# Moving 30 gathered expert rows from the second output projection and retrieval to the one-hot stage

## The chip, the cores and the metric

One core of a Trainium2 chip. The metric is the device time of one execution in microseconds, as the median of several runs. Differences of about 0.2% (5.5 us) and less can't be told from no change.

## What is computed

One layer of a hybrid encoder on 1024 tokens of width 1024, in float32: a mixing part (differential attention and a gated linear recurrence) with an output projection, and then PEER, a product-key retrieval of single-neuron experts, which this change concerns:

```
h = h + mix @ w_out
xt = rmsnorm(h, norm2_g)
q = (xt @ w_query).reshape(T, 8, 2, 128)
v1, i1 = top_k(q[:, :, 0] @ keys_1.T, 16); v2, i2 = top_k(q[:, :, 1] @ keys_2.T, 16)
sc, ci = top_k(v1[..., :, None] + v2[..., None, :], 16)
eid = i1[ci // 16] * 128 + i2[ci % 16]        # 8 heads x 16 = 128 experts for each token
act = gelu(einsum('thkd,td->thk', expert_down[eid], xt))
h = h + einsum('thk,thkd->td', softmax(sc) * act, expert_up[eid])
out = rmsnorm(h, norm_f_g)
```

There are 128 x 128 = 16384 experts, and each has a row of 1024 numbers in `expert_down` and one in `expert_up`.

## The kernel before

The tokens are cut into 8 blocks of 128. The first three (NG = 3) get their experts by **gathering rows**: for each of the 128 slots of a block GpSimd starts an indirect DMA that fetches one expert row for each of the 128 tokens (line 878, 512 KB in all), and VectorE takes it in with one instruction, for `expert_down` a product and sum against x2g (line 895), for `expert_up` a weighted addition to accg (line 905). That makes 3 x 2 x 128 = 768 rows. A row lands in one of five buffers of the pool `rows`, so a gather waits until the instruction that read its buffer is done. Line 728 at last scales a finished block.

The other five blocks (ND = 5) are **dense**: TensorE multiplies them by all of `expert_down` (`down_all`, tiles pd), the weights of the chosen experts are spread by one-hot matrices (`one_hots`, line 1135, and `weights`, tiles pg), and TensorE multiplies by all of `expert_up` (tiles pu); VectorE adds the sums to acc (line 1260), and the end norms the five blocks (lines 1266, 137 to 142 and 728).

After the first three blocks have chosen their experts, the program runs these stages: attention for the dense blocks; the second output projection (`for i in range(ND)`: two times eight matmuls into pa, line 997, an addition of x into h on VectorE, line 999, the square on ScalarE, line 1002, the multiplication to xt, line 1003, a reciprocal root of small instructions, a diagonal matrix diag, line 1006, and `turn`, which transposes and scales the block, line 982, and splits it into xdH and xdL, lines 126 and 127); the second retrieval (`query`, with `top_k_g` for the gathered blocks 1 and 2 beside it, index addition in line 932); a top-k for each dense block; the one-hot matrices; and the up stage.

The gathered rows are a generator, `gathered()`, and a stage takes steps of it by `gather_steps`. How many, the table G_ATT, G_OUT, G_QRY, G_TOPK, G_OH and G_UP says, and G_UP is what is left of 768:

```
gather_steps(G_OUT / (ND - G_LAST) if i < ND - G_LAST else 0)   # each block of the projection
gather_steps(G_QRY / (2 * PH))                                  # each of 16 query columns
gather_steps(G_OH * TB / (TD - OH_LAST) if t0 < TD - OH_LAST else 0)
gather_steps(G_UP / (n_steps - LAST))                           # each expert block of the up stage
gather_steps(2 * NG * SLOTS + 1)                                # what is left
```

This sets only where the steps stand in the program. The order on each engine is made when the program is built, by a planner that works out when each instruction could start and puts them in that order; row instructions are kept in their own order (`tc.keep_in_program_order`), and so are a few others. On the chip each engine then runs its list from first to last.

Of the kernel before, what the change touches and what calls it, by code (L numbers as in the profile page):

```python
# [47 lines left out]
TB = 16  # L48
TI = 2

G_ATT, G_OUT, G_QRY, G_TOPK, G_OH = 64, 24, 46, 0, 168
G_UP = 2 * NG * SLOTS - (G_ATT + G_OUT + G_QRY + G_TOPK + G_OH)
B_OUT, B_CHAIN, B_TURN, B_QRY, B_TOPK = 0, 3, 8, 8, 12
A_STEPS, A_AHEAD, A_FILL, LRU_AT, WO_AT = 3, 4, 0.5, 0.7, 50
# [1270 lines left out]
```

## Time and profile before

| | |
|---|---|
| median of 3 runs | 2761.29 us (2756.67 to 2762.64) |
| the profiled execution | 2766.01 us, its span 2764.2 us |
| TensorE (PE) busy | 2629.9 us, 95% of the span |
| VectorE (DVE) busy | 2274.7 us, 82% |
| ScalarE (ACT) busy | 1199.2 us, 43% |
| GpSimd (POOL) busy | 1093.7 us, 40% |
| DMA | 795.75 MB, 288 GB/s in the mean |

The span goes from the first to the last record of the profile, and the execution's own time is 1.8 us longer. Engines work side by side, so the shares don't add up to 100%. An instruction is named by its line, its output and its inputs, with buffer numbers left out.

### The profile page before, as it was taken

What the parts mean: (1) busy time and instruction counts of PE and PEld (TensorE: products, weight loads), DVE (VectorE), ACT (ScalarE), POOL (GpSimd) and SP (SyncE); (2) the same over time, 40 slices, a digit from 0 to 9 for tenths busy, and PEclk for the clock granted to TensorE, in tenths of its full rate; (3) what the DMA queues carried; (4) which work ended last, traced back from release to release, by engine and by line L of the source; (5) the groups of instructions that cost most, each with busy time, mean ns of one, the idle gap of its engine ahead of it and who ended that gap; (6) DMA issues with size and microseconds to landing.
All of it is one profiled execution on the core that took longest, in us unless ns stands there. A gap on an engine that the chain in (4) does not pass through costs nothing.

```text
span 2764.2 us, 43413 instructions
## 1 busy us (share of the span) xinstructions
PE 2629.9 (95%) x15577; PEld 2325.0 (84%) x15577; DVE 2274.7 (82%) x4737; ACT 1199.2 (43%) x2549; POOL 1093.7 (40%) x938
## 2 busy tenths in 40 slices
PE   7989978889999899999999999999999999999996
PEld 6767965746999899999998888888888888888885
DVE  6554879977999979998976788888888888888898
ACT  6653437632324657888862222222223222222222
POOL 2110236544231005443323455445444545545454
PEclk9989989989999999999999999999999999999998
DMA  6556999878684339999999999999999999999987
GB/s 194 139 134 205 319 208 267 240 262 300 213 285 147 115 128 336 358 348 330 340 373 335 324 336 321 342 333 355 337 332 339 341 331 327 346 345 326 349 295 260
DMA packets 321321, 795.75 MB, mean 288 GB/s; under 512 B 26208, under 2 KB 126576, under 8 KB 318544
## 3 DMA queue, kind: packets, MB, share of 16 engines
q0 software_dynamic: 141040, 442.44, 48.1%
q1 hardware_dynamic: 163248, 283.81, 30.4%
q10 hardware_dynamic: 16816, 66.72, 6.0%
q8 instruction: 122, 2.00, 0.3%
q14 instruction: 95, 0.78, 0.1%
HBM read 690.77 MB, written 102.11 MB: 287 GB/s over the span
## 4 chain that ended last, share of the span: by engine, by line
PE 77%; DVE 8%; DMA 7%; issue 4%; ACT 3%; POOL 1%; DVEq 0%; SPq 0%; ACTq 0%; POOLq 0%
PE pu L158 10%; PE pu L161 10%; PE pu L162 10%; PE pd L158 10%; PE pd L162 10%; PE pd L161 9%; PE pg L1159 4%; PE pa L158 3%; PE pa L162 2%; PE pa L161 2%; DMA row<-in_expert_up,eid 2%; PE pp L158 1%; PE pp L162 1%; PE pp L161 1%; PE pa L605 1%
## 5 line engine op out<-in xcount | busy, mean ns | idle before, releaser
L878 POOL DMA_INDIRECT row<-in_expert_up,eid x384 | 503.7, 1312 | 679.2 <-DVE accg L905 552.3
L878 POOL DMA_INDIRECT row<-in_expert_down,eid x384 | 492.7, 1283 | 570.0 <-DVE row L895 463.5
L158 PE MATMUL pd<-xdH,dh 128*128 128x320 f32 x2048 | 639.2, 312 | 3.7 <-ACT dh L126 3.3
L162 PE MATMUL pd<-xdH,dl 128*128 128x320 f32 x2048 | 631.5, 312 | 11.2 <-DVE dl L127 11.2
L161 PE MATMUL pd<-xdL,dh 128*128 128x320 f32 x2048 | 634.5, 310 | 0.0
L905 DVE SCALAR_TENSOR_TENSOR accg<-row,wg,accg 128x1024 f32<-128x1024 f32 x384 | 491.1, 1279 | 26.0 <-DMA row<-in_expert_up,eid 23.7
L161 PE MATMUL pu<-ul,w_h 128*128 128x512 f32 x1280 | 502.7, 393 | 1.0 <-DVE ul L127 1.0
L162 PE MATMUL pu<-uh,w_l 128*128 128x512 f32 x1280 | 498.5, 391 | 0.0
L895 DVE SCALAR_TENSOR_TENSOR row<-row,x2g 128x1024 f32<-128x1024 f32 x384 | 461.3, 1217 | 31.8 <-DMA row<-in_expert_down,eid 29.9
L162 PEld LDWEIGHTS pd<-xdH,dl 128*128 128x128 f32 x2048 | 385.6, 189 | 19.4 <-DVE dl L127 12.3
L158 PE MATMUL pu<-uh,w_h 128*128 128x512 f32 x1280 | 390.6, 393 | 9.5 <-DVE acc L1260 3.5
L158 PEld LDWEIGHTS pd<-xdH,dh 128*128 128x128 f32 x2048 | 387.4, 189 | 12.0 <-ACT dh L126 3.6
L161 PEld LDWEIGHTS pd<-xdL,dh 128*128 128x128 f32 x2048 | 387.2, 189 | 7.7
L126 ACT CAST uh<-uraw 128x512 fp32r<-128x512 f32 x256 | 157.9, 620 | 493.3 <-PE pu L162 395.8
L161 PEld LDWEIGHTS pu<-ul,w_h 128*128 128x128 f32 x1280 | 241.2, 188 | 49.0 <-DVE ul L127 2.2
L158 PEld LDWEIGHTS pu<-uh,w_h 128*128 128x128 f32 x1280 | 237.1, 189 | 53.1 <-issue 6.9
L162 PEld LDWEIGHTS pu<-uh,w_l 128*128 128x128 f32 x1280 | 240.6, 188 | 47.8
L126 ACT CAST dh<-draw 128x512 fp32r<-128x512 f32 x256 | 158.0, 618 | 248.9 <-PE pd L161 232.1
L127 DVE TENSOR_TENSOR ul<-uraw,uh 128x512 fp32r<-128x512 f32 x256 | 175.2, 686 | 73.9 <-ACT uh L126 72.4
L127 DVE TENSOR_TENSOR dl<-draw,dh 128x512 fp32r<-128x512 f32 x256 | 175.5, 686 | 71.9 <-ACT dh L126 67.1
L1146 ACT ACTIVATE o1a<-o,slot_a 128x128 bf16<-128x128 bf16 x640 | 194.4, 428 | 1.1 <-DVE o L1135 0.8
L126 ACT CAST w_h<-ga 128x640 fp32r<-128x640 f32 x128 | 93.0, 729 | 231.0 <-PE pu L161 138.3
(284 smaller groups left out, 4107.2 us busy)
## 6 DMA issues: line engine op xcount, KB each, us to landing
draw<-in_down_t SPq DMA_DIRECT2D x128, 512.0 KB
uraw<-in_up_h SPq DMA_DIRECT2D x128, 512.0 KB
gw<-gw_d SPq DMA_DIRECT2D x32, 1280.0 KB
gw_d<-st ACTq DMA_DIRECT2D x20, 1536.0 KB
act<-ga ACTq DMA_DIRECT2D x70, 320.0 KB
ga<-act SPq DMA_DIRECT2D x70, 320.0 KB
w_d<-w POOLq DMA_DIRECT2D x32, 512.0 KB
w<-w_d SPq DMA_DIRECT2D x32, 512.0 KB
```

The source lines that it names most:

```text
L126: A.copy(hi, src)
L127: (eng or V).tensor_sub(lo, src, hi.bitcast(F32))
L158: t = T.matmul(ps, wh, mh, start=first, stop=False)
L161: T.matmul(ps, wh, ml, start=False, stop=False)
L162: T.matmul(ps, wl, mh, start=False, stop=last)
L605: T.matmul(pss[:, t - t0, :], qt[:, t * P:(t + 1) * P], kt[:, ct % 2, :], start=True, stop=True)
L878: nc.gpsimd.indirect_dma_start(out=r, out_offset=None, in_=table, in_offset=bass.IndirectOffsetOnAxis(ap=eids[tb][:, s:s + 1], axis=0))
L895: tc.keep_in_program_order(V.scalar_tensor_tensor(r, r, 1.0, x2, op0=ALU.mult, op1=ALU.mult, accum_out=act[:, s:s + 1]))
L905: tc.keep_in_program_order(V.scalar_tensor_tensor(acc, r, w[:, s:s + 1], acc, op0=ALU.mult, op1=ALU.add))
L1146: A.activation(oa[:, g, :, j], o[:, g, 1, :, j], AF.Copy, scale=slot_a[b][:, tt + t:tt + t + 1])
L1159: T.matmul(ps[:, t - t4, :], o[:, g, 0, :, j], part[:, g, :, j], start=i == 0, stop=i == 2)
```

## The change

```
-G_ATT, G_OUT, G_QRY, G_TOPK, G_OH = 64, 24, 46, 0, 168
+G_ATT, G_OUT, G_QRY, G_TOPK, G_OH = 64, 0, 40, 0, 198
```

The 24 steps of the projection and 6 of the 46 steps of the queries go to the one-hot matrices. G_UP stays 466, and nothing else is edited. The order on the engines is made anew. Three places of it follow.

VectorE in the second output projection, around a block's two additions to h (line 999); L905 takes in a gathered row, n_v, n_r and n_t are the reciprocal root. Before:

```order
L999 TENSOR_TENSOR h<-pa,xt_5869 128x512
L905 SCALAR_TENSOR_TENSOR accg<-row,wg,accg 128x1024
L142 SCALAR_TENSOR_TENSOR n_r<-n_t,n_r 128x1
L905 SCALAR_TENSOR_TENSOR accg<-row,wg,accg 128x1024
L141 SCALAR_TENSOR_TENSOR n_t<-n_r,n_v 128x1
L905 SCALAR_TENSOR_TENSOR accg<-row,wg,accg 128x1024
L142 SCALAR_TENSOR_TENSOR n_r<-n_t,n_r 128x1
L905 SCALAR_TENSOR_TENSOR accg<-row,wg,accg 128x1024
L141 SCALAR_TENSOR_TENSOR n_t<-n_r,n_v 128x1
L142 SCALAR_TENSOR_TENSOR n_r<-n_t,n_r 128x1
L1006 TENSOR_SCALAR diag<-ident,n_r 128x128
L905 SCALAR_TENSOR_TENSOR accg<-row,wg,accg 128x1024
```

The same block in the change:

```order
L999 TENSOR_TENSOR h<-pa,xt_5819 128x512 x2
L1003 TENSOR_TENSOR xt_5819<-h,g2b 128x1024
L137 TENSOR_SCALAR n_v<-ss_5842 128x1
L138 TENSOR_SCALAR n_r<-n_v 128x1
L141 SCALAR_TENSOR_TENSOR n_t<-n_r,n_v 128x1
```

The row instructions between the block's own are gone.

VectorE at the first one-hot matrices with rows beside them (o and o1v are the matrices, dl a split of expert weights). Before:

```order
L1135 TENSOR_TENSOR o_10697<-key_t,slot_k_8428 128x4096
L127 TENSOR_TENSOR dl<-draw,dh 128x512
L905 SCALAR_TENSOR_TENSOR accg<-row,wg,accg 128x1024 x2
L127 TENSOR_TENSOR dl<-draw,dh 128x512
L905 SCALAR_TENSOR_TENSOR accg<-row,wg,accg 128x1024
L127 TENSOR_TENSOR dl<-draw,dh 128x512
L1139 TENSOR_TENSOR o1v<-o_10697,slot_w_8433 128x4096
```

The same in the change:

```order
L1135 TENSOR_TENSOR o_10614<-key_t,slot_k_8336 128x4096
L127 TENSOR_TENSOR dl<-draw,dh 128x512
L895 SCALAR_TENSOR_TENSOR row,actg<-row,x2g 128x1024 x5
L127 TENSOR_TENSOR dl<-draw,dh 128x512 x2
L1139 TENSOR_TENSOR o1v<-o_10614,slot_w_8341 128x4096
```

Here five rows stand in place of three, and they are earlier rows of the stream (`expert_up` rows before, `expert_down` rows now).

VectorE at the end, behind the third of the five last additions of TensorE's sums (line 1260, acc_16753 to acc_16757). Before:

```order
L1260 TENSOR_TENSOR acc_16755<-acc_16755,pu 128x512
L905 SCALAR_TENSOR_TENSOR accg<-row,wg,accg 128x1024 x2
L1260 TENSOR_TENSOR acc_16756<-acc_16756,pu 128x512
L905 SCALAR_TENSOR_TENSOR accg<-row,wg,accg 128x1024
L1260 TENSOR_TENSOR acc_16757<-acc_16757,pu 128x512
L1266 TENSOR_TENSOR ss_27911<-ssd 128x1
```

The same in the change:

```order
L1260 TENSOR_TENSOR acc_16755<-acc_16755,pu 128x512
L905 SCALAR_TENSOR_TENSOR accg<-row,wg,accg 128x1024 x2
L1260 TENSOR_TENSOR acc_16756<-acc_16756,pu 128x512
L905 SCALAR_TENSOR_TENSOR accg<-row,wg,accg 128x1024
L1260 TENSOR_TENSOR acc_16757<-acc_16757,pu 128x512
L905 SCALAR_TENSOR_TENSOR accg<-row,wg,accg 128x1024 x26
L1266 TENSOR_TENSOR ss_27911<-ssd 128x1
```

Between the last addition and the norms (line 1266) now stand 26 row instructions, where there was none.

## Rows read from the trace of the kernel before

**Rows 1.** The page's busy times, whole span (us, share, instructions).

```profile
PE 2629.9 (95%) x15577; PEld 2325.0 (84%) x15577; DVE 2274.7 (82%) x4737; ACT 1199.2 (43%) x2549; POOL 1093.7 (40%) x938
```

**Rows 2.** Busy time by stretch: length, engines (instructions), granted clock, DMA share, GB/s.

```profile
620.00:680.00 60.00, 56.97 (x217) 35.39 (x216) 49.34 (x85) 14.79 (x25) 30.02 (x25) 0.94 0.84 300
680.00:870.00 190.00, 188.59 (x1325) 188.32 (x1324) 175.72 (x892) 54.98 (x110) 47.13 (x37) 1.00 0.62 218
870.00:957.00 87.00, 78.14 (x519) 76.88 (x519) 85.24 (x428) 49.61 (x85) 11.68 (x10) 0.96 0.48 158
957.00:1417.00 460.00, 452.54 (x4165) 445.95 (x4164) 406.42 (x433) 374.20 (x1009) 169.85 (x114) 0.99 0.83 303
...
1460.00:2700.00 1240.00, 1236.45 (x6337) 1083.93 (x6338) 1041.99 (x1446) 348.92 (x606) 616.28 (x490) 1.00 0.95 334
```

**Rows 3.** The same view, gathered-row instructions alone; POOL (x) counts gathers.

```profile
620.00:650.00 30.00, 20.48 (x16) 0.00 (x0) 21.48 (x17) 1.00 0.93 328
...
957.00:1417.00 460.00, 144.23 (x147) 0.00 (x0) 169.85 (x114) 0.99 0.83 303
...
1460.00:2700.00 1240.00, 608.97 (x746) 1.14 (x2) 616.28 (x490) 1.00 0.95 334
```

**Rows 4.** VectorE's timeline at the end: start, duration, instruction, idle before and releaser.

```profile
2746.05 1.28 DVE L905 SCALAR_TENSOR_TENSOR accg<-row,wg,accg 128x1024 f32<-128x1024 f32 x1
2747.78 0.69 DVE L1260 TENSOR_TENSOR acc<-acc,pu 128x512 f32<-128x512 f32 x1 [0.45 <-PE pu L162]
...
2756.68 3.66 DVE L728 SCALAR_TENSOR_TENSOR acc<-acc,n_r,gfb 128x1024 f32<-128x1024 f32 x3
```

**Rows 5.** The page's costliest groups: rows added; busy, mean ns, idle before.

```profile
L905 DVE SCALAR_TENSOR_TENSOR accg<-row,wg,accg 128x1024 f32<-128x1024 f32 x384 | 491.1, 1279 | 26.0 <-DMA row<-in_expert_up,eid 23.7
```

**Rows 6.** Last 124.2 us: gather queue (packets, MB, share) and gathers (busy, mean ns).

```profile
q0 software_dynamic: 7056, 25.69, 60.5%
...
L878 POOL DMA_INDIRECT row<-in_expert_up,eid x49 | 63.5, 1297 | 40.6 <-DVE accg L905 32.6 <-issue 7.6 <-DMA row<-in_expert_up,eid 0.3
```

**Rows 7.** The chain that ended last, one row transfer: start, duration.

```profile
2707.67 6.62 DMA row<-in_expert_up,eid
```

**Rows 8.** GpSimd's timeline near the end.

```profile
2728.20 1.50 POOL L878 DMA_INDIRECT row<-in_expert_up,eid  x1 [0.30 <-issue]
...
2737.48 0.94 POOL L878 DMA_INDIRECT row<-in_expert_up,eid  x1 [0.65 <-DVE accg L905]
2739.28 1.86 POOL L878 DMA_INDIRECT row<-in_expert_up,eid  x1 [0.86 <-DVE accg L905]
```

**Rows 9.** Projection's last block: chain that ended last, then ScalarE's timeline.

```profile
660.53 0.46 DVE accg L905
...
664.33 1.22 DVE xt L1003
...
664.39 1.06 ACT L1002 ACTIVATE junk<-h 128x1024 bf16<-128x1024 f32 x1 [13.77 <-DVE h L999]
...
665.44 1.05 ACT L126 CAST xdH<-pt 128x512 fp32r<-128x512 f32 x2
```

**Rows 10.** TensorE's waits, 600 to 680, then 870 to 957: total, times, longest.

```profile
PE pa L158 <- ACT xdH L126: 2.9, 1, 2.9
...
PE ptk L1089 <- DVE cand L669: 6.2, 1, 6.2
```

**Rows 11.** Busy time by stretch, 5 us each.

```profile
665.00:670.00 5.00, 3.81 (x14) 3.47 (x15) 4.20 (x12) 3.13 (x7) 0.10 (x1) 0.56 0.97 314
670.00:675.00 5.00, 5.00 (x31) 5.00 (x31) 1.50 (x5) 0.73 (x2) 0.00 (x0) 0.76 0.58 233
675.00:680.00 5.00, 5.00 (x39) 5.00 (x38) 3.40 (x4) 1.46 (x3) 0.59 (x1) 1.00 0.00 0
```

**Rows 12.** VectorE's timeline, first and last of nine rows in the top-k.

```profile
876.50 1.22 DVE L895 SCALAR_TENSOR_TENSOR row<-row,x2g 128x1024 f32<-128x1024 f32 x1
...
898.80 1.26 DVE L905 SCALAR_TENSOR_TENSOR accg<-row,wg,accg 128x1024 f32<-128x1024 f32 x1
```

## The prediction

> **What bounds the kernel now.** I read the page's busy times first. TensorE is busy 95% of the span and VectorE 82% [rows 1], so a change can cost time in two ways only: by a wait of TensorE, or by work that stands alone once TensorE has finished.
>
> Next, the stretches by stage [rows 2]. In the second output projection (620 to 680 us) TensorE is busy 56.97 of 60 us, and in the second retrieval's queries (680 to 870) 188.59 of 190. In the top-k blocks (870 to 957) VectorE is busy 85.24 of 87 us and TensorE only 78.14: VectorE is the bound there. With the one-hot matrices (957 to 1417) and in the up stage (1460 to 2700) TensorE is the bound again.
>
> Third, where the gathered rows really run [rows 3]. GpSimd starts 17 gathers in the 30 us from 620, but only 114 in the 460 us of the one-hot matrices, where the table plans 168. In the up stage there are 490, where the table plans 466. So the table's numbers are not kept: the rows lag behind the plan and catch up late.
>
> Last, the end [rows 4]. The last gathered row is added at 2746.05 (until 2747.33), just ahead of the last addition of TensorE's sums (2747.78 to 2748.47). So the two streams end together now. Behind them come the norms and the output, to 2764.2.
>
> **The change part by part.** *What moves.* VectorE runs its instructions in a fixed order, so I counted the gathered-row instructions (lines 895 and 905) in both orders. When the first one-hot comparison (line 1135) is reached, 134 rows stand ahead of it before and 104 in the change; at the last one, 243 and 214. So between the first and the last comparison stand 109 and 110 rows: of the 30 rows that the table adds to that stage, the order takes one. Those that left the projection and the queries are not made up there, and the up stage holds no more than before either (from its first addition of TensorE's sums, with 271 and 248 rows ahead, to the last, 768 and 742: 497 and 494). The lag goes through to the end. Before, no row stands behind the last addition; now 26 do, in one run. The change does not do what its table says; that is read from the order and needs no guess.
>
> *The tail.* Those 26 rows run when TensorE is done, so all their time lies on the path. What does one row cost then? From below: the instruction itself, 1.279 us [rows 5], if the rows had all landed; but there are five buffers, so at most five have. Then the transfers: in the last 124.2 us the gather queue's packets took 60.5% of the 16 engines' time for 49 rows [rows 6], so 0.605 × 124.2 / 49 = 1.53 us for a row when nothing else moves. From above: with other transfers beside them, 17 rows took 30 us, 1.76 us for each, with DMA 0.93 busy [rows 3]. A third way gives the same: a row takes 6.62 us from its issue to its landing in a quiet moment [rows 7], then 1.279 us of VectorE, then 0.65 us till GpSimd starts the next gather into that buffer [rows 8]; 8.55 us for five buffers is 1.71 us for each. I take 1.70: the tail has gathers only, so it is under 1.76, but a buffer still has to go round. 26 × 1.70 = 44.2 us. A row that has already landed starts right after the last addition instead of before it, so the norms' chain starts 2748.47 - 2747.33 = 1.1 us later as well. Tail: 45.3 us; ends 1.53 × 26 + 1.1 = 40.9 and 1.76 × 26 + 1.1 = 46.9.
>
> How long GpSimd takes to start a gather is the doubtful part: single starts take from 0.94 to 1.86 us [rows 8], 1.297 in the mean of the last 49 [rows 6]. The Trainium skill (SBUF — State Buffer, section "SBUF: two separate sides") says that GpSimd and VectorE lock each other out of a shared port pair, for whole instructions, where a VectorE instruction has two inputs in SBUF and the GpSimd one reads SBUF; the row instruction has two and a gather reads its indices. By that rule the tail, where VectorE does little but such instructions, would run at the slow starts, which is rival B's time; the trace shows starts both of 0.94 and of 1.86 us beside row instructions, so it agrees at most in part.
>
> *The projection, given back.* Without the rows, VectorE's order there holds only the block's own work. Now the addition to h of the last block waits behind rows: the chain goes through a row at 660.53 and comes to xt, just behind h, at 664.33; ScalarE, idle for 13.77 us, starts the square at 664.39 and the cast of xdH at 665.44 [rows 9]; and TensorE waits 2.9 us for that cast [rows 10]. After it, the granted clock is 0.56 and 0.76 for 5 us each, against 1.00 elsewhere in the stage [rows 11]: between its two levels, (0.44 + 0.24) × 5 = 3.4 us lost. If all of it goes, that is 6.3 us; if the cast is late for another reason, nothing. TensorE's order is the same there, and the cast can never start before the turned block is there, so some wait stays: I take 4.
>
> *Queries and top-k, given back.* From the first row of the queries' part of the order to the one-hot matrices there are 44 rows before, 38 now. Where VectorE is the bound, behind the index addition of the second gathered block (line 932), there are 9 rows (876.50 to 900.0 [rows 12]) and now 2. 6 × 1.22 = 7.3 us less VectorE work in all, 7 × 1.22 = 8.5 in that stretch. But five of the remaining rows now stand just ahead of it, and TensorE also waits 6.2 us for the top-k itself [rows 10]. I take 5, ends 0 and 8.5.
>
> *One-hot matrices and up stage.* The same count of rows in both, TensorE the bound in both: nothing, covered by TensorE's 452.54 of 460 and 1236.45 of 1240 us [rows 2]. The block changes of the gathered rows (at row 256 and row 512) come a little later in the stream; if that cover were gone, they would cost a few us, inside the range.
>
> *Sum.* 45.3 - 4 - 5 = +36.3 us on the profiled execution, whose span of 2764.2 with 1.8 around it is 2766.0: 2802.3. That execution lies 4.7 above the median of 2761.3; on the median, 2797.6. From the bounds: 40.9 - 14.8 = +26.1 and 46.9 - 0 = +46.9, so 2787 to 2808 for this case alone.
>
> **The rivals.** *A, forecast:* as summed, 2797.6.
>
> *B, GpSimd sets the tail.* Each start takes 1.86 us with 0.30 between [rows 8], 2.16 for a row: 26 × 2.16 + 1.1 = 57.3; with only 3 given back, +54: 2815.6. For it: starts of 1.86 us are there. Against: the mean is 1.297, and in the stretch from 620 rows came at 1.76.
>
> *C, VectorE sets the tail.* Rows land as fast as they are added, 26 × 1.279 + 1.1 = 34.4, and all 14.8 come back: +19.6, 2780.9. Against: the transfers alone took 1.53 us for a row.
>
> *D, not slower.* TensorE gets back all that it loses between 620 and 1417: idle 3.0 + 1.4 + 8.9 + 7.5 = 20.8 us, and clock 0.06 × 60 + 0.04 × 87 + 0.01 × 460 = 11.7 us [rows 2], 32.5 in all, with C's tail: +1.9, 2763.2. It decides only if the last addition comes some 33 us earlier, by about 2715. Against: 7.5 us of that idle lie in the one-hot matrices, where the rows are as many as before, and the top-k's own waits stay.
>
> **How the numbers follow.** A 0.72, B 0.12, C 0.13, D 0.03. The likeliest is A: 2797.6. The range reaches from between C and A to near B, 2784 to 2812, and leaves out most of B, the lower half of C, and D. A measurement here can tell 0.2% (5.5 us) from no change. Faster by more than that would need D and more: 0.01. Within it, D: 0.02. Slower: 0.97.
>
> **What would show it.** Right: after the last matmul, TensorE is idle for some 60 us instead of 17; 26 row instructions stand there on VectorE with waits for row transfers between them, at 1.5 to 1.8 us for each; the chain that ended last has more of the row transfers; the last addition comes some 9 us earlier than 2748; TensorE's wait of 2.9 us and the low clock after it are smaller. Each step is wrong if: the rows at the end are 1.3 us apart (C) or over 2 (B); the last addition comes no earlier (nothing given back), or over 20 us earlier (D). The whole is wrong if there is no run of rows behind the last matmul.

## The result, and the profile after

The changed kernel takes **2803.35 us** (median of 4 runs, 2794.53 to 2804.37) against 2761.97 (4 runs, 2756.67 to 2766.49): a ratio of 1.014 (95% interval 1.0123 to 1.0158), +41.4 us where +36.3 was forecast. The profiled execution is the shortest of the four, 2794.53 us with a span of 2792.7. Its second output projection starts at 569.4 us, 8.7 us earlier than in the profile of before; the executions whose table has 64 in the attention spread from 569 to 579 us there. So the stages are compared by their lengths, not by clock times, and the stretches below, cut where [rows 2] are cut, hold up to 18 us of the stage behind.

The page's busy times and its groups of row additions and gathers, which answer to [rows 1] and [rows 5]:

```profile
PE 2622.0 (94%) x15577; PEld 2319.8 (83%) x15577; DVE 2277.1 (82%) x4737; ACT 1198.4 (43%) x2549; POOL 1117.1 (40%) x938
...
L878 POOL DMA_INDIRECT row<-in_expert_up,eid x384 | 513.7, 1338 | 622.2 <-DVE accg L905 515.2
...
L905 DVE SCALAR_TENSOR_TENSOR accg<-row,wg,accg 128x1024 f32<-128x1024 f32 x384 | 491.1, 1279 | 19.0 <-DMA row<-in_expert_up,eid 16.8
```

The work is the same; a row addition still takes 1279 ns. So the time is in where the rows stand. The busy times by stretch, with the columns of [rows 2]:

```profile
620.00:680.00 60.00, 58.94 (x296) 42.98 (x296) 25.04 (x84) 13.23 (x26) 0.00 (x0) 1.00 0.33 106
680.00:870.00 190.00, 184.36 (x1277) 183.77 (x1276) 181.14 (x904) 56.19 (x110) 45.28 (x36) 0.98 0.62 207
870.00:957.00 87.00, 79.99 (x543) 78.48 (x542) 84.21 (x379) 56.98 (x117) 2.12 (x3) 0.96 0.37 121
957.00:1417.00 460.00, 457.92 (x4257) 450.93 (x4257) 397.69 (x437) 370.00 (x985) 183.52 (x120) 1.00 0.86 318
1460.00:2700.00 1240.00, 1238.59 (x6351) 1085.81 (x6351) 1047.36 (x1459) 348.55 (x607) 638.69 (x494) 1.00 0.95 335
2700.00:2792.00 92.00, 29.49 (x119) 22.76 (x117) 72.77 (x115) 11.46 (x27) 48.60 (x37) 0.68 0.77 267
```

GpSimd starts no gather between 620 and 680 us (25 instructions there before), and the up stage's TensorE is as full as it was. The last row tells the rest: TensorE has 29.49 us of work in 92. VectorE's timeline there answers to [rows 4]:

```profile
2732.59 0.69 DVE L1260 TENSOR_TENSOR acc<-acc,pu 128x512 f32<-128x512 f32 x1 [0.44 <-PE pu L162]
2733.19 6.69 DVE L905 SCALAR_TENSOR_TENSOR accg<-row,wg,accg 128x1024 f32<-128x1024 f32 x5
2740.06 1.28 DVE L905 SCALAR_TENSOR_TENSOR accg<-row,wg,accg 128x1024 f32<-128x1024 f32 x1 [0.18 <-DMA row<-in_expert_up,eid]
2742.19 1.28 DVE L905 SCALAR_TENSOR_TENSOR accg<-row,wg,accg 128x1024 f32<-128x1024 f32 x1 [0.85 <-DMA row<-in_expert_up,eid]
2744.44 1.28 DVE L905 SCALAR_TENSOR_TENSOR accg<-row,wg,accg 128x1024 f32<-128x1024 f32 x1 [0.96 <-DMA row<-in_expert_up,eid]
2745.99 3.92 DVE L905 SCALAR_TENSOR_TENSOR accg<-row,wg,accg 128x1024 f32<-128x1024 f32 x3 [0.27 <-DMA row<-in_expert_up,eid]
...
2773.23 2.60 DVE L905 SCALAR_TENSOR_TENSOR accg<-row,wg,accg 128x1024 f32<-128x1024 f32 x2 [1.02 <-DMA row<-in_expert_up,eid]
2775.75 0.22 DVE L1266 TENSOR_TENSOR ss<-ssd 128x1 f32<-128x1 f32 x2
...
2785.18 3.67 DVE L728 SCALAR_TENSOR_TENSOR acc<-acc,n_r,gfb 128x1024 f32<-128x1024 f32 x3
```

After the last addition of TensorE's sums the 26 rows run alone, 2733.19 to 2775.75: 42.6 us, 1.64 for each. Five had landed and take 6.69 us; the other 21 take 35.9 us with 14 waits for transfers between them, 35.9 / 21 = 1.71 us each. From the last addition to the end are 60.1 us, 16.4 before.

GpSimd's timeline in the same place shows what the transfers wait for:

```profile
2739.68 1.02 POOL L878 DMA_INDIRECT row<-in_expert_up,eid  x1 [0.30 <-issue]
2741.00 1.16 POOL L878 DMA_INDIRECT row<-in_expert_up,eid  x1 [0.30 <-issue]
2742.46 1.83 POOL L878 DMA_INDIRECT row<-in_expert_up,eid  x1 [0.31 <-DMA row<-in_expert_up,eid]
2744.59 1.94 POOL L878 DMA_INDIRECT row<-in_expert_up,eid  x1 [0.30 <-DMA row<-in_expert_up,eid]
2746.84 1.25 POOL L878 DMA_INDIRECT row<-in_expert_up,eid  x1 [0.30 <-issue]
2748.39 1.01 POOL L878 DMA_INDIRECT row<-in_expert_up,eid  x1 [0.30 <-issue]
```

The starts follow one another with 0.30 us between. The same engine and line grouped, 2736.9 to 2771:

```profile
L878 POOL DMA_INDIRECT row<-in_expert_up,eid x20 | 27.1, 1357 | 6.1 <-issue 4.6 <-DMA row<-in_expert_up,eid 1.5
```

1.357 + 0.305 = 1.66 us for a start: GpSimd sets the pace of the tail, and none of these twenty waited for a buffer.

Ahead of the one-hot matrices the change gives time back. TensorE's waits in 600 to 680 us, which answer to [rows 10]:

```profile
PE pa L158 <- ACT xdH L126: 0.7, 1, 0.7
PE pt L982 <- DVE n_r L142: 0.3, 1, 0.3
```

and from the projection's end to the first one-hot comparison, before (676 to 957 us):

```profile
PE ptk L1089 <- DVE cand L669: 6.2, 1, 6.2
PE pd L162 <- DVE dl L127: 3.7, 2, 2.3
```

and after (662 to 940 us):

```profile
PE pd L162 <- DVE dl L127: 7.8, 4, 5.4
```

The wait for the cast fell from 2.9 to 0.7 us, with a granted clock of 1.00 from 620 to 680 us. In the queries and top-k the 6.2 us for the top-k (ptk) are gone, but TensorE now waits 7.8 us for splits of the expert weights (dl), where it waited 3.7 before: 9.9 us of these two waits became 7.8.

Between the last one-hot comparison and the up stage, where the prediction set nothing, some time is lost again. One of TensorE's waits from 1380 to 1480 us, then the stretch itself, and the matmuls of pd in it and in the up stage (TensorE, its weight loads, ScalarE); before:

```profile
PE pu L158 <- issue: 2.7, 1, 2.7
...
1401.90:1460.30 58.40, 52.41 (x432) 51.54 (x430) 32.99 (x41) 28.13 (x66) 13.60 (x12) 0.97 0.99 368
...
1401.90:1460.30 58.40, 44.51 (x288) 43.36 (x286) 4.33 (x10) 0.97 0.99 368
1460.30:2747.80 1287.50, 442.87 (x2674) 417.29 (x2674) 48.07 (x114) 1.00 0.94 332
```

and after:

```profile
PE pu L158 <- issue: 5.9, 1, 5.9
...
1384.40:1447.50 63.10, 53.80 (x442) 53.06 (x440) 35.52 (x36) 27.29 (x64) 21.40 (x17) 0.96 1.00 381
...
1384.40:1447.50 63.10, 45.90 (x298) 44.88 (x296) 4.35 (x10) 0.96 1.00 381
1447.50:2732.60 1285.10, 439.62 (x2664) 415.09 (x2664) 48.04 (x114) 1.00 0.94 333
```

17 gathers are started there instead of 12, the DMA engines have nothing left (1.00), and the stretch is 63.1 us long instead of 58.4. TensorE is idle for 9.3 us of it instead of 6.0; the rest of the difference is work that moved with the new order, ten matmuls of pd (298 for 288) that stood in the up stage before (2664 for 2674).

### The profile page after: what moved, and what is told of

It is laid out like the page before. It is cut to its first block, busy times and chain, and to the rows that moved or that the text cites. A ratio compares the mean times of both kernels' runs of the same rounds, so it can differ in the third digit from the quotient of the medians.

```text
span 2792.7 us, 43451 instructions
## 1 busy us (share of the span) xinstructions
PE 2622.0 (94%) x15577; PEld 2319.8 (83%) x15577; DVE 2277.1 (82%) x4737; ACT 1198.4 (43%) x2549; POOL 1117.1 (40%) x938
## 4 chain that ended last, share of the span: by engine, by line
PE 76%; issue 8%; DMA 6%; DVE 4%; ACT 3%; POOL 2%; SPq 0%; DVEq 0%; POOLq 0%; ACTq 0%
PE pu L158 10%; PE pu L161 10%; PE pu L162 10%; PE pd L158 8%; PE pd L162 8%; PE pd L161 8%; PE pg L1159 3%; PE pa L158 3%; PE pa L997 3%; PE pa L162 3%; PE pa L161 3%; PE pp L158 2%; PE pp L162 2%; PE pp L161 2%; POOL row L878 2%
## 5 line engine op out<-in xcount | busy, mean ns | idle before, releaser
L878 POOL DMA_INDIRECT row<-in_expert_up,eid x384 | 513.7, 1338 | 622.2 <-DVE accg L905 515.2
L878 POOL DMA_INDIRECT row<-in_expert_down,eid x384 | 506.2, 1318 | 628.7 <-DVE row L895 497.4
L905 DVE SCALAR_TENSOR_TENSOR accg<-row,wg,accg 128x1024 f32<-128x1024 f32 x384 | 491.1, 1279 | 19.0 <-DMA row<-in_expert_up,eid 16.8
## 6 DMA issues: line engine op xcount, KB each, us to landing
gw_d<-st ACTq DMA_DIRECT2D x20, 1536.0 KB, 10.4
```

The lines of the kernel that those rows point to most:

```text
L878: nc.gpsimd.indirect_dma_start(out=r, out_offset=None, in_=table, in_offset=bass.IndirectOffsetOnAxis(ap=eids[tb][:, s:s + 1], axis=0))
L905: tc.keep_in_program_order(V.scalar_tensor_tensor(acc, r, w[:, s:s + 1], acc, op0=ALU.mult, op1=ALU.add))
```

## The experiments

Where the text counts rows, it counts row instructions (lines 895 and 905) in the order of VectorE. Stages are measured from starts in each profiled execution: P from the first matmul of the second output projection to the first one-hot comparison, O to the last one-hot comparison, X to the first up matmul, U to the last addition of TensorE's sums, E to the end of the span (us; each mark was rounded to 0.1 us first, so a length can be 0.1 off).

| kernel | P | O | X | U | E |
|---|---|---|---|---|---|
| before | 377.9 | 445.9 | 58.4 | 1287.5 | 16.4 |
| before, again (b2) | 373.3 | 445.3 | 58.7 | 1289.7 | 16.5 |
| after | 370.0 | 445.0 | 63.1 | 1285.1 | 60.1 |
| e_cut | 370.0 | 445.7 | 63.2 | 1284.9 | 16.5 |
| e_half | 369.9 | 447.2 | 64.1 | 1285.2 | 53.0 |
| t_out | 369.4 | 454.7 | 63.3 | 1292.0 | 39.7 |
| t_qry | 379.1 | 442.6 | 62.4 | 1285.3 | 18.8 |
| t_qry70 | 396.0 | 445.0 | 58.4 | 1293.2 | 16.5 |
| t_att | 371.1 | 441.8 | 60.8 | 1283.1 | 15.3 |
| r_before | 377.3 | 444.2 | 51.5 | 1501.5 | 10.6 |
| r_after | 370.1 | 443.2 | 50.9 | 1515.1 | 10.4 |
| r_att40 | 376.4 | 444.8 | 51.5 | 1494.7 | 10.4 |
| r_att52 | 373.3 | 436.5 | 51.5 | 1501.5 | 10.4 |
| e_buf | 369.9 | 448.4 | 65.6 | 1364.0 | 13.8 |

**Is the loss the tail? (e_cut)** The changed kernel without its last 26 rows of `expert_up` for the third gathered block, which are left out of its sum:

```
-                for s in range(g * GRP, (g + 1) * GRP):
+                for s in range(g * GRP, (g + 1) * GRP - (26 if tb == NG - 1 and g == SLOTS // GRP - 1 else 0)):
```

> The change with the last 26 rows of the third gathered block left out (its last 26 expert_up rows are neither fetched nor added), so nothing stands behind the last addition of TensorE's sums; every engine's order ahead of it is that of the change. Theory (the loss is the run of 26 rows at the end): the time falls by 26 x 1.63 + 1 = 43 us from the change, to 2755 to 2762, that is 0 to 7 us under the kernel before. Rival (the loss is spread over the one-hot matrices and the up stage, where the rows are later than before): it stays above 2790. If the time given back ahead of the end were the 9 us of the prediction, it is 2753.

2760.99 us (2756.61 to 2766.12, 10 runs), ratio 0.9997 (0.9985 to 1.0009). Without the tail nothing of the loss is left, as the theory had it: in the net the whole +41 us is those 26 rows, and what the change gives and takes ahead of them comes to nothing that can be measured. A net gain of 9 us elsewhere, which would give 2753, is outside the interval (-4.1 to +2.5 us).

**How much does the projection give back? (b2)** The kernel before once more, unedited.

> The kernel before once more, for a second profile. Theory (TensorE's wait of 2.9 us at the projection's last block, the low clock behind it and the length of the top-k are the order's doing): from the first matmul of the projection (line 997) to the first one-hot comparison it takes 378 us again, within 2 us, with the wait. Rival (part of what the change seemed to give back there is that one execution's own): 374 us or less, without the wait or with a shorter one.

2754.65 us (one run). P was 373.3 us against 377.9, so the theory missed on the length; yet the wait for xdH was there again, as TensorE's waits in 600 to 680 us show:

```profile
PE pa L158 <- ACT xdH L126: 2.5, 1, 2.5
```

The granted clock behind it did not fall this time, as the busy times by stretch show:

```profile
655.00:660.00 5.00, 3.84 (x28) 3.61 (x28) 4.77 (x15) 2.88 (x7) 0.00 (x0) 1.00 0.98 332
660.00:665.00 5.00, 5.00 (x41) 5.00 (x40) 1.95 (x3) 2.18 (x4) 0.00 (x0) 1.00 0.60 240
```

In r_before (below), which has the same rows in the projection, it did:

```profile
660.00:665.00 5.00, 2.99 (x11) 2.64 (x12) 4.54 (x12) 3.38 (x7) 0.92 (x1) 0.58 1.02 365
665.00:670.00 5.00, 5.00 (x29) 5.00 (x29) 1.87 (x5) 0.93 (x2) 0.00 (x0) 0.74 0.65 257
```

So the wait belongs to the order, and the low clock of [rows 11] follows it in some executions and not in others. Six profiled executions have the projection's rows in place: all wait for the cast, 2.4 to 5.1 us, and behind it the clock falls in four (before, t_qry, r_before, r_att40) and not in two (b2, r_att52). In the eight with the projection emptied the wait is 0.7 us and no clock falls behind it. With the order of before P was 377.9, 373.3 and 377.3 (r_before); with the change's, 370.0, 370.0, 369.9 and 370.1. Given back: 3 to 8 us, 7 by the middle of the three. Cut at the last block's turn (last matmul of line 982), the projection took 98.2 and 94.1 us in the two executions of before, 92.2 in after and e_cut; the rest, to the first one-hot comparison, 279.7 and 279.2 against 277.7 and 277.8. So the projection gives back 2 to 6 us, by whether the clock fell (over all six and eight executions 96.3 against 92.2 in the mean, 4.1), and the queries and top-k 1.4 to 2.0.

**What sets the pace at the end? (e_half)** The last 26 row instructions work on half the columns (the other half is left out), so VectorE is busy for a shorter time and the gathers are as they were:

```
+                    n = 512 if tb == NG - 1 and s >= SLOTS - 26 else D
...
-                        acc, r, w[:, s:s + 1], acc, op0=ALU.mult, op1=ALU.add))
+                        acc[:, :n], r[:, :n], w[:, s:s + 1], acc[:, :n], op0=ALU.mult, op1=ALU.add))
```

> The change with the last 26 row instructions cut to half of the columns (the other half of these 26 expert_up rows is not added); the gathers fetch whole rows as before, and the order is that of the change. In the change GpSimd starts the gathers of the end back to back, 1.33 us each with 0.30 between, 1.63 us a row. Theory (a start that falls into a row instruction of VectorE waits for its end, so shorter instructions make shorter starts): the starts fall to 1.1 to 1.2 us in the mean and the rows come at 1.45 to 1.55, the time falls by 2 to 5 us to 2799 to 2801. Rival 1 (transfers or the five buffers set the pace): the starts are followed by waits for buffers, the pitch stays at 1.55 to 1.63. Rival 2 (VectorE's instructions set it): the pitch falls by 0.6 to about 1.0, the time by 15 us.

2794.03 us (2 runs), ratio 1.0114 (1.0089 to 1.0138). GpSimd's timeline, then VectorE's:

```profile
2751.72 0.94 POOL L878 DMA_INDIRECT row<-in_expert_up,eid  x1 [0.34 <-DVE accg L906]
2753.00 0.94 POOL L878 DMA_INDIRECT row<-in_expert_up,eid  x1 [0.34 <-DVE accg L906]
2754.38 0.94 POOL L878 DMA_INDIRECT row<-in_expert_up,eid  x1 [0.44 <-DVE accg L906]
```

```profile
2751.98 0.75 DVE L906 SCALAR_TENSOR_TENSOR accg<-row,wg,accg 128x512 f32<-128x512 f32 x1 [0.53 <-DMA row<-in_expert_up,eid]
2753.36 0.75 DVE L906 SCALAR_TENSOR_TENSOR accg<-row,wg,accg 128x512 f32<-128x512 f32 x1 [0.63 <-DMA row<-in_expert_up,eid]
```

Each start now takes 0.94 us, and all but the first begin where VectorE is idle; the rows come 35.4 / 26 = 1.36 us apart, and GpSimd waits for buffers instead. The busy times of the tail, first of e_half:

```profile
2738.00:2770.00 32.00, 0.00 (x0) 0.00 (x0) 17.62 (x24) 0.72 (x2) 20.71 (x23) 0.56 0.99 376
```

then of the change:

```profile
2733.00:2769.00 36.00, 0.00 (x0) 0.00 (x0) 28.42 (x23) 0.72 (x2) 29.06 (x22) 0.55 0.90 305
```

The DMA engines rise from 0.90 to 0.99. So the slow starts were VectorE's doing, and behind them lies a second limit near 1.36 us for a row, of transfers and five buffers together; the two were not separated. None of the three expectations has this pitch, or the 9.3 us by which the time fell: the starts shortened by more than the theory said, and the waits for buffers of rival 1 came at a lower price.

**The projection's 24 rows alone (t_out)**

```
-G_ATT, G_OUT, G_QRY, G_TOPK, G_OH = 64, 24, 46, 0, 168
+G_ATT, G_OUT, G_QRY, G_TOPK, G_OH = 64, 0, 46, 0, 192
```

> Only the 24 rows of the projection move to the one-hot matrices (table 64, 0, 46, 0, 192). By the built order 14 rows stand behind the last addition. Theory (each row there costs 1.63 us, the emptied projection gives back 2 to 5): 2762 + 14 x 1.63 + 1 - 3 = 2783, within 2779 to 2788. Rival (the loss goes by the number of rows that the table moves, 24 of 30 of 41 us): 2795.

2792.58 us (2790.03 to 2795.06, 4 runs), ratio 1.0105 (1.0087 to 1.0124): a miss for the theory, near the rival's figure, though not by its mechanism. The order has 14 rows at the end and E is 23.3 us longer, as expected. The rest comes from O (+8.8), X (+4.9) and U (+4.5), less 8.5 in P. In O some 35 matmuls of the expert weights (pd), 5.1 us, stand that ran in the top-k before: what the top-k stage gave back in this run was partly work that moved (in the change itself none did: 944 matmuls of pd stand in P before and after).

**The queries' 6 rows alone (t_qry)**

```
+G_ATT, G_OUT, G_QRY, G_TOPK, G_OH = 64, 24, 40, 0, 174
```

> Only the 6 rows of the queries move to the one-hot matrices (table 64, 24, 40, 0, 174). By the built order one row stands behind the last addition. Theory: 2762 + 2 + 1 less 0 to 5 for the shorter VectorE work in the top-k: 2760 to 2765. Rival (by the number of rows moved, 6 of 30 of 41 us): 2770.

2767.05 us (2765.39 to 2773.54, 10 runs), ratio 1.0026 (1.0015 to 1.0037), between the two. One row stands at the end (E +2.4), X is 4.0 longer, and nothing is given back in P (379.1). Nor could it be: 133 rows stand ahead of the first one-hot comparison in this order, 134 before, so of the six rows that the table moves one left. Further on 238 stand ahead of the last comparison instead of 243, so that the rows lag into X. What the six rows cost in the queries this run doesn't show.

**More rows in the queries (t_qry70)**: the projection's rows go to the queries.

```
+G_ATT, G_OUT, G_QRY, G_TOPK, G_OH = 64, 0, 70, 0, 168
```

> The projection is emptied as in the change, but its 24 rows go to the queries and not to the one-hot matrices (table 64, 0, 70, 0, 168). By the built order no row stands behind the last addition, and 66 rows stand between the projection and the one-hot matrices, where there were 44 before. Theory (no run of rows at the end, so no such loss; the 22 more rows cost what VectorE has no idle time for, 22 x 1.22 = 27 less the 14 us of idle time in the queries): 2762 - 3 + 13 = 2772, within 2758 to 2786. Rival (an emptied projection costs the rows' time wherever they go): 2800.

2787.39 us (2785.2 to 2790.07), ratio 1.0087 (1.007 to 1.0103), just over the theory's range. The order has no row at the end, but P is 18 to 23 us longer. The stretch from 870 us to its end:

```profile
870.00:975.00 105.00, 79.17 (x523) 77.16 (x522) 101.82 (x484) 51.56 (x89) 19.06 (x16) 0.92 0.49 164
```

VectorE is busy 101.82 of 105 us. From the projection's end to the first one-hot comparison 66 row instructions run instead of 46, and it takes 303.8 us, 24 more: here a row costs its whole instruction. In the projection the change has 21 row instructions fewer (14 for 35) and gains 2 to 6 us, 0.3 each at most: that was their cheap place.

**More rows in the attention (t_att)**

```
+G_ATT, G_OUT, G_QRY, G_TOPK, G_OH = 88, 0, 46, 0, 168
```

> The 24 rows of the projection go to the attention ahead of it (table 88, 0, 46, 0, 168). By the built order 80 rows stand ahead of the projection's first addition (61 before), 88 ahead of its last, and the order behind it holds the same counts as before; no row behind the last addition. Theory (what counts is that the stream has room for its rows by the end, and no row stands at the end): 2757 to 2766. Rival (an emptier projection and later rows cost as in the change): 2780 or more.

2778.36 us (2777.0 to 2779.96), ratio 1.0056 (1.0037 to 1.0075): the theory missed. No row at the end, P 2 to 7 us shorter, but the projection starts at 605.0 us, where the kernels with 64 in the attention's number have 569 to 579, 574.5 in the mean. Two of TensorE's waits from 100 to 605 us:

```profile
PE ps L245 <- ACT e L253: 29.1, 13, 8.8
...
PE pt L302 <- DVE o_sb L289: 9.5, 1, 9.5
```

In the kernel before these are 22.0 and 2.9 us; the two make up 13.7 of the 30 us, and the rest was not followed. The attention has no room for 24 rows more: 30 / 24 = 1.25 us for each that the table moves. Fewer rows there give time back: with 40 and 52 in that number (r_att40 and r_att52 below) the projection starts at 558.5 and 559.9 us, 16 and 15 us earlier.

**More buffers at the end (e_buf)**: the change's table, with the last 26 steps behind the loop and 8 of those rows in the buffers of the `expert_down` loads (draw).

```
-G_UP = 2 * NG * SLOTS - (G_ATT + G_OUT + G_QRY + G_TOPK + G_OH)
+G_UP = 2 * NG * SLOTS - 26 - (G_ATT + G_OUT + G_QRY + G_TOPK + G_OH)
...
-            r = rows.tile([P, D], F32, name="row")
+            r = dp.tile([P, D], F32, name="rowd", tag="draw", bufs=RAWS) if more else rows.tile([P, D], F32, name="row")
...
+                    r = gather(expert_up, tb, s, tb == NG - 1 and s >= SLOTS - 26 and s % 7 < 2)
```

> The table of the change; of the last 26 rows 8 land in two buffers of the up stage that held expert weights (draw) in place of the five of the rows, and the last 26 steps stand behind the loop in the program. By the built order no row then stands behind the last addition. Theory (the lag comes of the planner's five buffers, and rows that find a place beside TensorE's matmuls cost nothing): the loss goes, 2755 to 2765. Rival (the rows cost their time wherever they are, or the borrowed buffers hold up the expert weights): 2780 or more.

2838.93 us (2829.8 to 2842.63), ratio 1.0266 (1.0239 to 1.0294), as the rival had it. The rows did move ahead of the last sums, but TensorE's waits from 1400 us on show the price:

```profile
PE pd L158 <- ACT dh L126: 80.0, 2, 76.2
```

A borrowed buffer is lost to its owner: the expert weights came 76.2 us late once. A sixth buffer of its own has no room beside the kernel's other tiles and wasn't tried, so whether five buffers are why the order lets the rows lag is not shown.

**Rows spread evenly over the up stage (r_before, r_after, r_att40, r_att52)**. The one-hot number is set to the 110 rows that the order puts there anyway, the remainder goes to the up stage, and the splits of its weights keep their place among the rows, so that the planner can't put them ahead:

```
-        (eng or V).tensor_sub(lo, src, hi.bitcast(F32))
+        t = (eng or V).tensor_sub(lo, src, hi.bitcast(F32))
+        if pin:
+            tc.keep_in_program_order(t)
...
-                    split(raw, uh, ul)
+                    split(raw, uh, ul, pin=True)
...
+G_ATT, G_OUT, G_QRY, G_TOPK, G_OH = 64, 24, 46, 0, 110
```

This is r_before; r_after has 64, 0, 40, 0, 110, r_att40 40, 24, 46, 0, 110 and r_att52 52, 24, 46, 0, 110.

> The kernel before, with the splits of the up stage's expert weights (ul) kept in program order among the rows, and the one-hot number of the table set to the 110 rows that the order gives that stage anyway, so that the other 58 stand in the up stage's number. Rows ahead of the first and last one-hot comparison are 134 and 242, ahead of the first and last addition of the up stage 260 and 768, none behind it. Theory (it is the planner putting rows behind the up stage's splits that lets them lag; spread evenly they cost the same): 2761, within 6. Rival (an even spread holds up the weights' splits): 2770 or more.

> The change's table with the one-hot number at 110 and the up stage's splits in program order, so that the 30 rows and the lag land in the up stage instead of behind it: 104 and 213 rows ahead of the one-hot comparisons, 231 and 768 ahead of the first and last addition of the up stage, none behind it. Theory (the loss of the change is the row run at the end alone, and the up stage has some 60 us of its 1240 in which the DMA engines are free against 40 more rows at 1.53): 2753 to 2763, the first one-hot matrices 3 to 8 us earlier. Rival (the up stage is at the limit of its transfers, so that the rows cost there what they cost at the end): 2785 or more, TensorE waiting in the up stage for buffers or weights.

> 24 rows less in the attention (40 in place of 64), the projection and queries of the kernel before, one-hot number 110, splits of the up stage in program order: 110 and 218 rows ahead of the one-hot comparisons, 237 and 768 ahead of the up stage's additions, none behind. Theory (a row in the attention costs about 1.25 us, as 24 more of them cost 30 us, one in the up stage nothing as long as the transfers fit): 2730, 2724 to 2745. Rival (531 rows are over what the transfers of the up stage take beside the weights): 2750 to 2775.

> As the one before with 12 rows less in the attention (52): 122 and 230 rows ahead of the one-hot comparisons, 249 and 768 ahead of the up stage's additions. Theory: half the gain, 2745, 2738 to 2753. Rival of the transfers' limit: 2750 or more, but nearer to the kernel before than the one with 40.

2957.04, 2967.43, 2945.63 and 2943.34 us; ratios 1.07 (1.0672 to 1.0728), 1.0744 (1.0726 to 1.0762), 1.0675 (1.0648 to 1.0702) and 1.0675 (1.0645 to 1.0704). All four theories missed by some 200 us; the rivals of the first two, with the weights held up, had the direction. The tail is gone, E is even 6 us shorter, and the up stage is 214 us longer in r_before. TensorE's waits there, from 1400 us:

```profile
PE pu L163 <- DVE ul L127: 71.7, 41, 6.1
PE pu L160 <- ACT uh L126: 39.3, 11, 6.8
PE pu L160 <- DVE acc L1262: 17.3, 16, 2.5
```

In the kernel before the wait for ul is 1.0 us in the whole program. In all, TensorE is idle for 143 us of this up stage against 8 before, and it is busy for 1359 us against 1280, at a granted clock of 0.95 in the mean against 1.00. A split that stands behind rows comes late, and TensorE waits with it. That the lag of the rows is what the planner pays to have the weights early fits this, but the table and the splits' order were changed together, and no run separates them. The four don't answer whether the up stage could hold 30 more rows, since it was disturbed in all of them. None of the versions run here beats both kernels.

## Why the prediction was right, and where it was off

- *What moves.* Right: the counts of rows in the order, 26 at the end, are what the trace shows. The table's one-hot number adds next to nothing to that stage, as counted (110 rows for 109).
- *The tail.* Right in size: 45.3 forecast, E +43.7 measured (60.1 - 16.4), of which the rows are 42.6. The step that failed is the reason: "a buffer still has to go round". Of twenty starts in the tail none waits for a buffer; the starts follow one another at 1.66 us, which is rival B's mechanism at a lower price (2.16 was taken, with every start slow). That the buffers' 1.71 came so near is luck; GpSimd's own rows already gave 1.297 + 0.30 = 1.60 [rows 6, rows 8]. Nor was 1.53 what the transfers need "when nothing else moves": its stretch held the expert weights' transfers too, and in e_half rows came at 1.36.
- *Given back ahead of the one-hot matrices.* For the projection 4 was forecast and 2 to 6 measured, 4.1 in the mean: of the 6.3 that were its upper end, 2.2 of the cast's 2.9 us went, and the 3.4 us of low clock go only where an execution had them. The step that failed is "I take 5" for queries and top-k: 1.4 to 2.0. The rows left VectorE and the wait for the top-k (ptk) of 6.2 us is gone, but the waits for dl grew from 3.7 to 7.8 us in the same stage.
- *One-hot matrices and up stage: nothing.* The step that failed: the transition between the two, X, lies for the most part between the two stretches that the forecast named (to 1417 and from 1460 us), and TensorE idles there for 9.3 us instead of 6.0. Its idle time goes with the gathers that start in X: 1.0 us with one or two (the four r_ runs, which differ in the splits too), 6.0 to 6.5 with twelve (before, b2, t_qry70, t_att), 8.2 to 12.0 with 16 or 17 (t_out, t_qry, after, e_cut, e_half, e_buf). With the DMA engines at 0.99 to 1.00 there was no cover to count on. That the rows' transfers hold up weights of the up stage there fits; which load is late was not singled out. The other 1.4 us of X's 4.7 are the ten matmuls of pd, which left U.
- *Sum.* Tail +43.7, P -7, O -0.9, X +4.7, U -2.4 is +38, against +41.4 measured with an interval of +34.0 to +43.6. The forecast's +36.3 lies in that interval: the terms that were off partly cancel.

Rivals: C falls (1.71 us for a waiting row, not 1.28). D falls: the last addition came at 2732.59, 4 and 15 us earlier than in the two executions of before (2736.4 and 2747.8), where 33 were needed. B is right in what sets the pace and wrong in its price.

## What to carry to other kernels

A number in a source table is not an order: count the instructions of a stream in the order that the engines got, stage by stage, and look at what stands behind the last one. Background work that lags shows most of its cost at the end, where each piece costs its full pace (here 1.64 us a row, against 0.3 at most in the projection, a whole instruction of 1.2 where VectorE is the bound, and 1.25 for each that the table adds to the attention), so it is best taken where the engine that does it has room, even if TensorE pays a little for it. And a stretch with the DMA engines at 0.99 covers no more gathers, short as it is.

## What the runs showed of the hardware that was not expected

A gather's start on GpSimd takes 0.94 us in e_half's tail (22 of 22, of which all but the first begin while VectorE is idle and the first 0.06 us into a row instruction) and 1.01 to 1.97 in the twenty of the change's tail. There the end is tied to VectorE: the row instruction that starts at 2742.19 ends at 2743.47, and the gather that began under it at 2742.46 ends at 2744.29, 0.82 us later; with the next pair (2744.44 and 2744.59) it is 0.81. This is so in the whole program: of the change's 768 gathers 200 begin under a row instruction, and their median end is 0.81 us after it. The 32 that begin under an addition of TensorE's sums (line 1260), which has one of its inputs (pu) in PSUM, all take 0.93 to 0.94. So a start that falls into a row instruction seems to do most of its work after that instruction is over. The other way round nothing shows: the 26 row instructions sum to 33.4 us, 1.286 each, and in the kernel before line 905 takes 1.278 us in the mean where a gather is running as it starts (221 times) and 1.280 where none is (163).

The Trainium skill (SBUF — State Buffer, section "SBUF: two separate sides") says that a VectorE instruction with two inputs in SBUF and a GpSimd instruction that reads SBUF exclude each other on a shared pair of ports, and that the later of them waits for the whole of the other. On GpSimd's side these runs agree, with 0.94 us against up to 1.97; on VectorE's side no row instruction of the tail took over 1.33 us. The prediction took the start of 0.94 us at 2737.48 [rows 8] as one beside a row instruction and let the rule agree "at most in part". VectorE's timeline of the kernel before shows that it began under an addition of TensorE's sums, and the one of 1.86 us at 2739.28 under a row:

```profile
2737.13 0.68 DVE L1260 TENSOR_TENSOR acc<-acc,pu 128x512 f32<-128x512 f32 x1
2737.73 2.60 DVE L905 SCALAR_TENSOR_TENSOR accg<-row,wg,accg 128x1024 f32<-128x1024 f32 x2
```

What made rival B's price too high is that a start is longer only by what is left of the row instruction: the twenty of the tail take 1.357 us in the mean.
